# RWKV element stage of a two-layer encoder trunk: ten chunks at once on VectorE, b and k of both heads packed, 64x64 products, inverses of two head pairs together

## The chip, the cores and the metric

One core of a Trainium2 chip (trn2) runs the whole program. The metric is device time in microseconds: the median of several executions. One more execution is recorded by the hardware profiler; its span, from the first to the last instruction, is what the rows below are counted in.

## The reference

The kernel computes one inference step of a trunk of two layers (width 1024) in float32: an even layer with a pooling mixer and differential attention, an odd layer with RWKV-7 time mixing, in both layers cross attention and SwiGLU behind the mixer, and a final norm. There are 512 tokens of a prompt and 8 sequences of 16 tokens of a sample, 640 columns together. What matters here is the recurrence of the odd layer, for 16 heads of size 64:

```
kk = heads(k * k_k); kk = kk / max(norm(kk), 1e-12)
k  = k * (1 + (a - 1) * k_a);  decay = exp(-exp(w))
def step(S, inp):
    r_t, d_t, k_t, v_t, kk_t, a_t = inp
    sa = einsum('bhvk,bhk->bhv', S, -kk_t)
    S = S * d_t + sa[..., None] * (kk_t * a_t) + v_t[..., None] * k_t
    return S, einsum('bhvk,bhk->bhv', S, r_t)
xs = (r, decay, k, v, kk, a) over time
S_fin, y = lax.scan(step, S0, xs)
```

## The kernel before, in words

Features lie on the partitions and the 640 tokens on the free axis; a tile of 128 features holds two heads, a head pair `m` (0 to 7). Large products (`block_steps`, written by `mm`, line 224) split weights and inputs into a high and a low part and take three products of 128x128 weights with 320 columns for each block. `load_w` makes the parts: ScalarE rounds (`wh`, line 241), VectorE or GpSimd subtracts (`wl`).

SBUF is cut into 59 numbered slots of 656 columns (kind `t`) and 22 of 256 (`n`), PSUM into 8 banks; a tile that takes a slot waits for the work on that slot alone. All `dma_start` calls of the RWKV stage except a few outputs are issued by SyncE, one queue in program order. The order of instructions on each engine is made by the framework's scheduler, which runs the program in a timeline simulation and goes by priorities; the priorities follow the order in which the code is written.

The recurrence is computed in chunks of 64 tokens (8 chunks of the prompt, 2 of the sample). For every head pair `rw_elem` makes from the projections `k`, `r` and the low-rank inputs the running decay (`up`, line 1452, a scan), its reciprocal `pi`, the in-context rate `am`, the normed key `kn`, and of these `zr` = (-kk P(t-1) | r P) and `bk` = (b = kk a / P | k (1 + (a-1) k_a) / P), all as [128 features, chunk, 2, 64]. `zr` lies in two tiles of five chunks (a ring of three), `bk` in two tiles a head and five chunks each, where the rows of the other head hold zeros (three sets, `bks`). VectorE writes `zr` in eight instructions and the `b` half of `bk` in four; GpSimd multiplies `kn` by `am`, `am` by `k`, and writes the `k` half of `bk` in four. Then come, for groups of four, four and two chunks, the products (b | k)^T (z | r) with 128x128 weights (line 1510), masked by VectorE into `gm` and stored by SyncE into the DRAM scratch `d_gb` and `d_w` (lines 1514 and 1515); `zr` goes to `d_w` (line 1501), and the transposes of `bk` (line 1524) go over ScalarE (line 1526) to `d_bt` (line 1527).

`inverse` (one head pair) reads 16x16 blocks back from `d_gb` with eight DMAs (line 1539), inverts them, one block on each of 80 partitions, in a loop of 15 steps of one multiplication and one sum on VectorE (lines 1547 and 1548), stores them (line 1549), reads them back in another layout, and joins them to 32x32 and 64x64 blocks with small products into `p_l` and VectorE and ScalarE steps, down to `mt` (lines 1597 to 1600). Its temporaries are one buffer each, so a loop ends before the next pair's blocks are loaded.

Between these steps `pace` puts pieces of a large product as a filler: the rest of the receptances for the first pairs, then the values (`gemm_tok_steps`). `elem` starts the first part of the next pair (to the `yield`) ahead of the second part of the present one. When all eight pairs are done, `chunk` runs the chunks of two groups of four pairs, each hanging on the state of the one before, with `sample`, `y_norm` and the gates between them.

Of the kernel before, what the change touches and what calls it, by code (L numbers as in the profile page):

```python
# [9 lines left out]
F32 = mybir.dt.float32  # L10
# [16 lines left out]
NSLOT = 59  # L27
# [3 lines left out]

class Held(list):
    """tiles that stay until they are given back"""
# [3 lines left out]
class Trunk:  # L37
    """The tiles of SBUF and PSUM lie in numbered slots of one size, a tag each, so that what waits for
    a slot waits for the work on that slot alone. Slots are taken the longest free first."""
# [5 lines left out]
    XV = 9  # L45
# [9 lines left out]
    IB = [1, 1, 1, 1]  # L55
# [29 lines left out]
    def ring(self, kind, name, n, dt):  # L85
        """a temporary: the next of the n slots that the name has in this scope"""
# [123 lines left out]
    def split(self, hl, src, scale=None, eng=None):  # L210
        """hl = the two float32r parts of src (times a per-partition scale)."""
# [20 lines left out]
    def load_w(self, src, kb, cols, rows=128):  # L232
        """src: DRAM view [rows, kb, cols], or pieces ((c0, c1), view) of one; returns its float32r parts."""
# [34 lines left out]
    def gemm(self, hl, w2d, ncols, evac, r0=0, c0=0, halves=HALVES, first=()):  # L268
        """first: parts of the first blocks of weights, when they are there already"""
# [11 lines left out]
    def gemm_tok(self, hl, w2d, c0, ncols, ntiles, evac, nb=None):  # L281
        """tokens on the partitions, two tiles of them a bank, nb banks at once: evac(i, c, psum [128, 256])"""
# [26 lines left out]
    def constants(self):  # L309
# [15 lines left out]
        # rows (h, m, t) -> (h, t)  # L325
# [3 lines left out]
        # selectors of partition bits: bit 16  # L329
# [3 lines left out]
        # sequence selector of rows s (mod 64) // 16  # L333
# [3 lines left out]
        # heads of a pair: features to head rows and back  # L337
# [4 lines left out]
        # iota on the free dim and row index  # L342
# [7 lines left out]
        # masks of the chunk: [strict | inclusive]  # L350
# [8 lines left out]
        # reciprocal counts of the first positions  # L359
# [3 lines left out]
        # the scan starts anew behind each of these columns  # L363
# [5 lines left out]
    def columns(self):  # L369
        """vectors over features as columns"""  # L370
# [38 lines left out]
        # lambda  # L409
# [11 lines left out]
        # 1 on the rows of the first map, -lambda on those of the second  # L421
# [14 lines left out]
    def load_x(self):  # L436
        """the transposes follow in turn_x"""
# [33 lines left out]
    def rms(self, role, pool=True):  # L471
        """1 / rms of the tokens: [128, 5] with tokens on the partitions, and as rows on all partitions"""
# [26 lines left out]
    def normed(self, gcol):  # L499
        """float32r parts of x * gain; 1 / rms is applied behind the product"""  # L500
# [10 lines left out]
    def even(self):  # L511
# [48 lines left out]
        # scores of the samples' new keys, a column block a sequence  # L560
# [8 lines left out]
        # outputs: new keys and values  # L569
# [18 lines left out]
        with self.scope():  # L588
            # history of the pool
# [87 lines left out]
    def softmax_rows(self, p, s, name):  # L677
        """exp(s - max) into p, returns 1 / sum"""
# [8 lines left out]
    def diff_prompt(self, h, q, k, vt, out):  # L687
        """one head of the prompt: out [128, (token tile, e)], normalised by the first map's sum"""
# [3 lines left out]
        for i in range(4):  # L692
# [20 lines left out]
            # p0 - lambda p1, over the sum of p0  # L713
# [12 lines left out]
    def sub_ln(self, tiles, name):  # L726
        """groups of 128 columns of the tiles [128, 512], in place: over their rms"""
# [1194 lines left out]
```

## Time and profile before

| | |
|---|---|
| median of 3 runs | 2436.52 us (2433.37 to 2438.97) |
| span of the profiled execution | 2428.2 us; the page gives no other time of it |
| TensorE matmuls, share of the span | 94% |
| VectorE, ScalarE, GpSimd | 53%, 34%, 22% |
| DMA | 280.42 MB, mean 115 GB/s |

Busy time is time in which an engine executes an instruction; issues of DMAs, waits and semaphores are not counted. Matmuls are pipelined and their ends modelled, so the sum of a group's durations is more than its busy time. A float32 matmul with both operands unrounded is recorded as two. Some matmul records are missing from a trace. The granted TensorE clock is 1.00 at 2.4 GHz and 0.50 at 1.2 GHz; a stretch between has had some of both. A line of the code can be a helper's: all plain elementwise products of VectorE and GpSimd have line 205, those with a scalar 208, all matmuls but transposes 224.

### The profile page before, as it was taken

The page shows a single profiled execution, that of the slowest core. Times are in us where ns is not written, and L with a number is a line of the kernel's source. Part 1 is how long each engine was busy: PE and PEld are TensorE (multiplying, and loading weights), DVE is VectorE, ACT ScalarE, POOL GpSimd, SP SyncE. Part 2 cuts the span into 40 slices and gives each one's busy share as a digit, 9 for nine tenths or more (in the row PEclk, how much of TensorE's full clock was granted, in tenths as well). Part 3 has the DMA queues.
Part 4 walks back from the last instruction along what each step waited for, and adds up shares of the span by engine and source line. Part 5 has one row for each costly group of instructions (what it writes and reads, how often), then busy time and mean ns, then how long its engine had stood idle before and what let it go on. Part 6 is the DMA issues. An engine that isn't in the chain of part 4 may idle for free. (4 is left out here: it accounts for less than half of the span.)

```text
span 2428.2 us, 45754 instructions
## 1 busy us (share of the span) xinstructions
PE 2281.2 (94%) x18943; PEld 2119.8 (87%) x18943; DVE 1284.7 (53%) x2361; ACT 814.5 (34%) x1493; POOL 525.4 (22%) x536
## 2 busy tenths in 40 slices
PE   8998999999999999979998987696999999999998
PEld 7886999789999999978887876574997899999997
DVE  4467543454434424484759886579444544344344
ACT  4335432333212212366734432222323432122122
POOL 2122220012101102244555322233200212011010
PEclk9999999999999999999997878797999999999999
DMA  3218644423222222453245556674445222222222
GB/s 120 74 62 295 204 136 148 160 77 87 74 75 79 71 87 73 135 163 91 74 128 149 145 138 157 183 204 118 135 132 165 65 79 72 77 79 81 76 72 77
DMA packets 428322, 280.42 MB, mean 115 GB/s; under 512 B 79130, under 2 KB 383535, under 8 KB 428114
## 3 DMA queue, kind: packets, MB, share of 16 engines
q1 hardware_dynamic: 424513, 268.01, 38.0%
q0 software_dynamic: 3600, 9.49, 1.1%
q8 instruction: 149, 2.44, 0.4%
q14 instruction: 60, 0.48, 0.1%
HBM read 231.22 MB, written 46.20 MB: 114 GB/s over the span
## 5 line engine op out<-in xcount | busy, mean ns | idle before, releaser
L224 PE MATMUL p_g<-xn,wh 128*128 128x320 f32 x3712 | 721.6, 310 | 0.4 <-DVE xn L208 0.4
L224 PEld LDWEIGHTS p_g<-xn,wh 128*128 128x128 f32 x3712 | 588.7, 188 | 9.8 <-issue 8.4
L241 ACT CAST wh<-wr 128x1024 fp32r<-128x1024 f32 (+3 forms) x279 | 272.8, 978 | 861.7 <-PE p_g L224 534.0
L224 PE MATMUL p_g<-xn,wl 128*128 128x320 f32 x1856 | 444.1, 310 | 3.3 <-DVE wl L205 3.3
L205 DVE TENSOR_TENSOR wl<-wr,wh 128x1024 fp32r<-128x1024 f32 (+2 forms) x251 | 305.6, 1218 | 73.9 <-ACT wh L241 57.2
L224 PEld LDWEIGHTS p_g<-xn,wl 128*128 128x128 f32 x1856 | 316.2, 188 | 7.0 <-DVE wl L205 3.7
L224 PE MATMUL p_g<-hid,wh 128*128 128x320 f32 x1408 | 264.8, 309 | 0.0
L205 POOL TENSOR_TENSOR gate<-gate,sgate 128x320 f32<-128x320 f32 x88 | 118.1, 1363 | 676.1 <-DVE gate L205 517.6
L205 DVE TENSOR_TENSOR gate<-p_g,rstd 128x320 f32<-128x320 f32 x176 | 78.3, 486 | 327.5 <-PE p_g L224 324.8
L205 DVE TENSOR_TENSOR x<-x,p_g 128x320 f32<-128x320 f32 x192 | 85.5, 483 | 281.6 <-PE p_g L224 281.5
L224 PEld LDWEIGHTS p_g<-hid,wh 128*128 128x128 f32 x1408 | 221.4, 188 | 0.0
L224 PE MATMUL p_g<-hid,wl 128*128 128x320 f32 x704 | 161.4, 310 | 0.0
L224 PE MATMUL p_g<-mixr,wh 128*128 128x320 f32 (+2 forms) x640 | 128.4, 313 | 3.1 <-ACT wh L241 2.6
L224 PEld LDWEIGHTS p_g<-hid,wl 128*128 128x128 f32 x704 | 117.6, 188 | 0.0
L224 PE MATMUL p_g<-xohl,wh 128*128 128x320 f32 x512 | 110.0, 319 | 4.8 <-ACT xohl L214 4.7
L224 PEld LDWEIGHTS p_g<-mixr,wh 128*128 128x128 f32 (+2 forms) x640 | 98.5, 179 | 11.6 <-issue 5.6
L205 POOL TENSOR_TENSOR acc<-acc,sq 128x640 f32<-128x640 f32 x36 | 66.2, 1840 | 146.3 <-ACT sq L202 146.1
L224 PEld LDWEIGHTS p_g<-xohl,wh 128*128 128x128 f32 x512 | 82.4, 188 | 9.9 <-ACT xohl L214 7.0
L948 POOL TENSOR_SCALAR xp<-xp,xsm 128x256 f32<-128x256 f32 x32 | 15.3, 478 | 305.6 <-DVE xsm L684 299.6
L224 PE MATMUL p_g<-mixr,wl 128*128 128x320 f32 (+2 forms) x320 | 78.0, 314 | 0.0
L205 POOL TENSOR_TENSOR wl<-wr,wh 128x1024 fp32r<-128x1024 f32 (+2 forms) x28 | 64.4, 2301 | 60.4 <-ACT wh L241 57.2
L205 DVE TENSOR_TENSOR hid<-gate,hid 128x320 fp32r<-128x320 f32 x88 | 72.1, 819 | 7.8 <-ACT hid L214 7.8
(485 smaller groups left out, 3836.4 us busy)
## 6 DMA issues: line engine op xcount, KB each, us to landing
wr<-in_ffn_wg SPq DMA_DIRECT2D x44, 512.0 KB
wr<-in_ffn_wu SPq DMA_DIRECT2D x44, 512.0 KB
kc<-in_cache_mem_k SPq DMA_DIRECT2D x64, 256.0 KB
vc<-in_cache_mem_v SPq DMA_DIRECT2D x64, 256.0 KB
wr<-in_ffn_wd SPq DMA_DIRECT2D x32, 512.0 KB
wr<-in_ev_w_in SPq DMA_DIRECT2D x16, 512.0 KB
wr<-in_xa_wk SPq DMA_DIRECT2D x16, 512.0 KB
kc<-in_cache_diff_k SPq DMA_DIRECT2D x32, 256.0 KB
```

Of the source, the lines that this page charges most:

```text
L205: (eng or self.nc.vector).tensor_tensor(out, a, b, op=op)
L224: self.nc.tensor.matmul(out, lhsT, rhs, start=start, stop=stop, **kw)
L241: nc.scalar.copy(wh[0:rows, 0:n], wr[0:rows, 0:n])
L948: nc.gpsimd.tensor_scalar(p, p, rs, 1.0, op0=ALU.mult, op1=ALU.mult)
```

## The change

- The elementwise part of a head pair works over all ten chunks at once. `zr` and `bk` are one tile of 1280 columns each, two buffers each of their own (`wide`), outside the numbered slots. `zr` takes four instructions; the products of `kn`, `am`, `k` and `pi` are four instructions of VectorE over 128x640; GpSimd has none of them.
- `bk` holds b and k of both heads without zeros. Each product of a chunk is four matmuls of 64x64 weights: head `h` reads partitions 64h.., and half `e` (b or k) writes the PSUM rows `half(h, e)`.
- `zr` is stored by two DMAs instead of four; `bt` by nine instead of three, as the second head's halves come out in the other order.
- The second part of the low-rank products and the key direction's product take 128 rows with zeros in place of 64 rows (`wz`, two tiles; two `rn` tiles, one a group).
- `inverse` takes two head pairs: sixteen loads of blocks, one loop over [80, 2, n, n], joins of 16 chunks. It follows every odd pair.
- The numbered slots go from 59 to 56, the ring of `vc` in the cross attention from 9 to 8 tiles, GpSimd's DMA scratch to 4096. The inverses of the first group are given back after its last chunk.

```diff
-NSLOT = 59
+NSLOT = 56
+BACC = dict(dynamic_dma_scratch_size=4096)
-    XV = 9
+    XV = 8
+    def wide(self, tag, name):
+        return self.sb.tile([128, 1280], F32, tag=tag, name=name, bufs=1)
...
-            yield from self.rw_elem(m, r, k, rns[0][0][f, 0:NT], selT[m % 4 // 2][0][f, c:c + 128], low_in, sp)
+            yield from self.rw_elem(m, r, k, rns[m // 4][0][:, 0:NT], selT[m % 4 // 2][0][:, c:c + 128], low_in, sp)
...
-            inv[m] = self.inverse(m, sp, nsv[m // 4][:, m % 4])
+            if m % 2:
+                inv[m - 1:m + 1] = self.inverse(m - 1, sp, [nsv[i // 4][:, i % 4] for i in (m - 1, m)])
...
+        wz = self.wz[m % 2]
+        for i in range(2):
+            r = slice(64 * i, 64 * i + 64)
+            nc.scalar.copy(wz[r, i * 128:(i + 1) * 128], ws[r, i * 128:(i + 1) * 128])
...
-            self.mm(p[:, 0:n], wa[r, i * 128:(i + 1) * 128], low[2][r, t0:t0 + n], start=False, stop=True)
+            self.mm(p[:, 0:n], wz[:, i * 128:(i + 1) * 128], low[2][:, t0:t0 + n], start=False, stop=True)
...
-        self.stt(zr[0][:, :, 0, :], ch(kn[:, 0:320]), -1.0, P[:, 0:5, 0:64])
-        self.stt(zr[1][:, 0:3, 0, :], ch(kn[:, 320:512]), -1.0, P[:, 5:8, 0:64])
-        self.tt(zr[0][:, :, 1, :], ch(r_[:, 0:320]), P[:, 0:5, 1:65])
-        self.tt(zr[1][:, 0:3, 1, :], ch(r_[:, 320:512]), P[:, 5:8, 1:65])
...
+        self.stt(zr[:, 0:8, 0, :], ch(kn[:, 0:512]), -1.0, P[:, :, 0:64])
+        self.tt(zr[:, 0:8, 1, :], ch(r_[:, 0:512]), P[:, :, 1:65])
+        self.stt(z4(0), s4(kn[:, 512:640]), -1.0, p4(S[:, :, 0:16]))
+        self.tt(z4(1), s4(r_[:, 512:640]), p4(S[:, :, 1:17]))
...
-        self.tt(kn, kn, am, eng=nc.gpsimd)
+        self.tt(kn, kn, am)
         self.act(am, am, AF.Identity, scale=c1("rw_k_a"), bias=self.ka1[:, m:m + 1])
-        self.tt(am, am, k, eng=nc.gpsimd)
-        for i in range(2):
-            for h in range(2):
...
-                self.tt(bk[i][h][r, :, h, :], ch(kn[r, s]), ch(pi[r, s]))
-                self.tt(bk[i][h][r, :, 1 - h, :], ch(am[r, s]), ch(pi[r, s]), eng=nc.gpsimd)
+        self.tt(bk[:, :, 0, :], ch(kn), ch(pi))
+        self.tt(am, am, k)
+        self.tt(bk[:, :, 1, :], ch(am), ch(pi))
...
+        half = lambda h, e: slice(64 * (e ^ h), 64 * (e ^ h) + 64)
...
-                for h in range(2):
-                    i = (c0 + c) // 5
-                    self.mm(pg[h][:, c * 128:(c + 1) * 128], piece(bk[i][h], c0 + c), piece(zr[i], c0 + c))
+                for e in range(2):
+                    for h in range(2):
+                        self.mm(pg[h][half(h, e), c * 128:(c + 1) * 128], bk[hs(h), c0 + c, e, :],
+                                zr[hs(h), c0 + c].rearrange("p z t -> p (z t)"))
...
-            nc.sync.dma_start(out=sp["bt"][c0:c0 + nch, :, m, :].rearrange("c p f -> p c f"), in_=bt)
+                for src, dst in ((half(0, 0), half(1, 0)), (half(0, 1), half(1, 1))) if h else ((slice(0, 128), slice(0, 128)),):
+                    nc.sync.dma_start(out=sp["bt"][c0:c0 + nch, dst, m, f].rearrange("c p f -> p c f"), in_=bt[src, :, f])
...
-            t = T[:, 0:n * n].rearrange("p (t j) -> p t j", t=n)
-            self.tt(t, Nv[:, s + 1:16, s + 1:16].rearrange("p j t -> p t j"), Xv[:, s, s + 1:16].unsqueeze(1).to_broadcast([nb, n, n]))
-            nc.vector.tensor_reduce(Nv[:, s, s + 1:16], t, axis=AX.X, op=ALU.add)
+            t = T[:, 0:2 * n * n].rearrange("p (i t j) -> p i t j", i=2, t=n)
+            self.tt(t, Nv[:, :, s + 1:16, s + 1:16].rearrange("p i j t -> p i t j"),
+                    Xv[:, :, s, s + 1:16].unsqueeze(2).to_broadcast([nb, 2, n, n]))
+            nc.vector.tensor_reduce(Nv[:, :, s, s + 1:16], t, axis=AX.X, op=ALU.add)
```

## Rows read from the trace of the kernel before

**Rows 1.** The page: the span, and busy us and share by engine.

```profile
span 2428.2 us, 45754 instructions
...
PE 2281.2 (94%) x18943; PEld 2119.8 (87%) x18943; DVE 1284.7 (53%) x2361; ACT 814.5 (34%) x1493; POOL 525.4 (22%) x536
```

**Rows 2.** Busy us by stretch: PE, PEld, DVE, ACT, POOL, granted clock, DMA share, GB/s.

```profile
1205.00:1275.00 70.00, 69.79 (x493) 62.36 (x492) 39.27 (x67) 28.09 (x53) 37.35 (x36) 1.00 0.45 119
1275.00:1475.00 200.00, 173.63 (x2107) 150.99 (x2105) 169.75 (x389) 78.97 (x172) 79.31 (x91) 0.81 0.57 144
...
1500.00:1660.00 160.00, 130.27 (x2334) 102.73 (x2334) 103.38 (x235) 41.97 (x103) 37.06 (x31) 0.84 0.71 199
```

**Rows 3.** Instructions of three lines: ns min/median/max, first and last start us, shapes.

```profile
L1452 DVE TENSOR_TENSOR_SCAN u<-rst,u x8: 1510/1522/3210, 1215.7 to 1443.1; 128x656 f32<-128x656 f32 x8
...
L1549 SPq DMA_DIRECT2D d_np<-in x8: 329/430/522, 1309.7 to 1517.4; - x8
...
L1600 ACT COPY mt<-p_l x16: 344/362/363, 1337.8 to 1536.6; 32x256 f32<-32x256 f32 x16
```

**Rows 4.** Waits of PE, 1275 to 1475 us, the longest: us, times, longest.

```profile
PE p_f L224 <- DVE kn L208: 7.4, 5, 3.7
```

**Rows 5.** DVE groups, 1205 to 1540 us (busy us, mean ns), and one of `rn`.

```profile
L205 DVE TENSOR_TENSOR bk<-kn,pi 64x320 f32<-64x320 f32 x32 | 30.1, 941 | 3.8 <-POOL kn L205 3.3
...
L205 DVE TENSOR_TENSOR it<-in,ix 80x225 f32<-80x225 f32 x8 | 4.3, 538 | 0.2
...
L1548 DVE TENSOR_REDUCE in<-it 80x15 f32<-80x225 f32 x8 | 3.0, 376 | 0.1
...
L205 DVE TENSOR_TENSOR it<-in,ix 80x1 f32<-80x1 f32 x8 | 1.2, 147 | 5.3 <-DMA ix<-d_gb 3.5 <-DMA d_v<-vtok 1.4 <-issue 0.4
L1548 DVE TENSOR_REDUCE in<-it 80x1 f32<-80x1 f32 x8 | 1.2, 146 | 0.2
...
L205 DVE TENSOR_TENSOR rn<-krst,rn x2: 816/819/822, 1153.6 to 1198.2; 32x640 fp32r<-32x640 f32 x2
```

**Rows 6.** DVE alone, 1205 to 1540 us: sums for `zr`, then for the loops.

```profile
sum 335.00, DVE 21.83; mean DVE 7.28
...
sum 335.00, DVE 77.59; mean DVE 25.86
```

**Rows 7.** POOL groups, 1205 to 1540 us: busy us, mean ns, idle before.

```profile
L205 POOL TENSOR_TENSOR bk<-am,pi 64x320 f32<-64x320 f32 x32 | 33.4, 1045 | 2.4
L205 POOL TENSOR_TENSOR wl<-wr,wh 128x1024 fp32r<-128x1024 f32 x14 | 33.2, 2376 | 30.2 <-ACT wh L241 27.0 <-PE p_g L224 3.0
L205 POOL TENSOR_TENSOR kn<-kn,am 128x640 f32<-128x640 f32 x8 | 12.4, 1551 | 34.1 <-DVE zr L208 25.1 <-DVE in L1548 8.9
```

**Rows 8.** The timeline of DVE and of POOL: start us, us, instructions merged.

```profile
1327.08 4.98 DVE L205 TENSOR_TENSOR bk<-kn,pi 64x320 f32<-64x320 f32 x4
...
1328.54 4.25 POOL L205 TENSOR_TENSOR bk<-am,pi 64x320 f32<-64x320 f32 x4
```

**Rows 9.** PE groups, 1205 to 1540 us; last, `p_e` alone by stretch.

```profile
L224 PE MATMUL p_f<-zr,bk 128*128 128x128 f32 x320 | 56.9, 335 | 1.1 <-DVE gm L205 1.0
...
L224 PE MATMUL p_g<-mixr,wh 128*128 128x320 f32 x226 | 48.6, 317 | 0.2 <-DVE krst L194 0.2
...
1275.00:1475.00 200.00, 25.10 (x54) 0.81 0.57 144
```

**Rows 10.** PE groups, 1500 to 1660 us: busy us, mean ns, idle before.

```profile
L224 PE MATMUL p_c<-u,mt 64*64 64x64 f32 x240 | 13.6, 234 | 0.5 <-ACT mt L1600 0.5
...
L224 PE MATMUL p_x<-S,wcs 64*32 64x128 f32 x256 | 10.5, 300 | 0.3 <-ACT S L192 0.3
```

**Rows 11.** Issues on SyncE's queue: ns min/median/max, first and last start us.

```profile
L1539 SPq DMA_DIRECT2D ix<-d_gb x64: 739/756/972, 1261.6 to 1501.2; - x64
...
L1501 SPq DMA_DIRECT2D d_w<-zr x32: 575/626/791, 1233.8 to 1461.8; - x32
...
L1527 SPq DMA_DIRECT2D d_bt<-am x16: 364/536/1399, 1262.6 to 1491.0; - x16
```

More of the change, by code (lines that the diff above doesn't have):

```diff
@@ L54 @@
     CP = '01s01sn01s01sn0101Gn01Y01n'
-    IB = [1, 1, 1, 1]
     AH = 1
@@ L1291, in rwkv @@
         self.banks(g=(0, 1), f=(2, 3, 4, 5), l=(6,), e=(7,))
-        bks = self.take(6, "bk")
-        self.bk = [[t[:, 0:NT] for t in bks[2 * i:2 * i + 2]] for i in range(3)]
-        for b in self.bk:
-            for h in range(2):
-                nc.gpsimd.memset(b[h][64 - 64 * h:128 - 64 * h], 0.0)
+        wzs = self.take(2, "wz", "n", dt=F32R)
+        self.wz = wzs
+        for t in wzs:
+            nc.gpsimd.memset(t[64:128, 0:128].bitcast(F32), 0.0)
+            nc.gpsimd.memset(t[0:64, 128:256].bitcast(F32), 0.0)
         with self.scope():
@@ L1323, in step @@
                     todo.append((g, c // 2))
+                if c == 7 and g == 0:
+                    self.give(*inv[0:4])
             if self.CV < 8:
@@ L1396, in rwkv @@
         self.give(*yh)
-        self.give(*inv, ns)
+        self.give(*inv[4:8], ns)
         yo = self.hl(8, "yo")
@@ L1533, in inverse @@
         nb = 80
-        X, N = [self.n(nm, self.IB[0])[0:nb] for nm in ("ix", "in")]
-        T = self.n("it", self.IB[1])[0:nb]
-        for b in range(8):
-            h, q = b // 4, b % 4
-            r = slice(64 * h + 16 * q, 64 * h + 16 * q + 16)
-            nc.sync.dma_start(out=X[b:nb:8].rearrange("c (s t) -> c s t", s=16), in_=sp["gb"][:, r, m, 16 * q:16 * q + 16])
+        X, N, T = [self.t(nm, 1)[0:nb, 0:512] for nm in ("iX", "iN", "iT")]
+        for i in range(2):
+            for b in range(8):
+                h, q = b // 4, b % 4
+                r = slice(64 * h + 16 * q, 64 * h + 16 * q + 16)
+                nc.sync.dma_start(out=X[b:nb:8, 256 * i:256 * i + 256].rearrange("c (s t) -> c s t", s=16),
+                                  in_=sp["gb"][:, r, m + i, 16 * q:16 * q + 16])
@@ L1557, in inverse @@
-        mt = self.take(1, "mt")
-        M = mt[0][:, 0:512].rearrange("p (c t) -> p c t", c=8)
+            t = T[:, 0:2 * n * n].rearrange("p (i t j) -> p i t j", i=2, t=n)
+            self.tt(t, Nv[:, :, s + 1:16, s + 1:16].rearrange("p i j t -> p i t j"),
+                    Xv[:, :, s, s + 1:16].unsqueeze(2).to_broadcast([nb, 2, n, n]))
+            nc.vector.tensor_reduce(Nv[:, :, s, s + 1:16], t, axis=AX.X, op=ALU.add)
+        n16 = self.n("n16", 1)
+        gz, mts = [], []
+        for i in range(2):
+            nc.sync.dma_start(out=sp["np"][m + i].rearrange("c b s t -> (c b) (s t)"), in_=N[:, 256 * i:256 * i + 256])
+            nv = sp["np"][m + i].rearrange("c b s t -> (b s) c t")
+            nc.sync.dma_start(out=n16[:, 128 * i:128 * i + 128].rearrange("p (c t) -> p c t", c=8), in_=nv[:, 0:8])
+            nc.sync.dma_start(out=ns[i], in_=nv[:, 8:10])
+            gz.append(self.t("gz")[:, 0:512].rearrange("p (c t) -> p c t", c=8))
+            nc.sync.dma_start(out=gz[i], in_=sp["gb"][0:8, :, m + i, 0:64].rearrange("c p f -> p c f"))
+            mts.append(self.take(1, "mt"))
@@ L1574, in inverse @@
+        Y = NI
+        self.tt(Y, p, NI, ALU.subtract)
         p = self.ps("l")
-        for c in range(8):
+        for c in range(16):
             for r in quads:
                 self.mm(p[r, o(c)], Y[r, o(c)], N[r, o(c)])
-        self.tt(T, N, p[:, 0:256], ALU.add)
+        T = N
+        self.tt(T, N, p, ALU.add)
         tt_, Y2 = NT_, Y
@@ L1582, in inverse @@
         p = self.ps("l")
-        for c in range(8):
+        for c in range(16):
             for h in range(2):
                 a, b_ = quads[2 * h], quads[2 * h + 1]
-                self.mm(p[b_, o(c)], gz[a, c, 32:64], tt_[a, o(c)], tile_position=(64 * h, 64 * h + 32))
+                self.mm(p[b_, o(c)], gz[c // 8][a, c % 8, 32:64], tt_[a, o(c)], tile_position=(64 * h, 64 * h + 32))
         for h in range(2):
             b_ = quads[2 * h + 1]
-            nc.scalar.copy(Y2[b_], p[b_, 0:256])
+            nc.scalar.copy(Y2[b_], p[b_])
         p = self.ps("l")
-        for c in range(8):
+        for c in range(16):
             for h in range(2):
```

96 lines of the change are left out of this document (43 added, 53 removed).

## The prediction

> **What bounds the kernel now.** I read the shares of the span first, then the busy time by stretches. TensorE is busy 94% of the 2428.2 us [rows 1], so outside one part nothing but fewer matmuls could shorten the kernel. That part is the RWKV mixer. Up to 1275 us its element stage runs under TensorE work without a gap: 69.79 of 70 us busy, clock 1.00. From 1275 to 1475 TensorE is busy 173.63 of 200 us with a granted clock of 0.81, that is, a good part of the stretch at 1.2 instead of 2.4 GHz, while VectorE is busy 169.75 of 200 us and GpSimd 79 [rows 2]. No engine is full; each waits on the others in turn. The head pairs follow each other at a steady pace: the scan (one a pair) starts at 1215.7 and for the eighth time at 1443.1 us, so a period is 227.4 / 7 = 32.5 us [rows 3]. The longest wait of TensorE here is for `kn`, which VectorE makes [rows 4]. The chain of waits of the whole kernel covers only its last microseconds and says nothing of this stage.
>
> Why VectorE is slow is seen when its rows are held against GpSimd's. A quarter-product of `bk` on VectorE takes 941 ns in the mean, though it has 64x320 elements and one of 32x640 needs 819 [rows 5]. In the timeline four of them last 4.98 us beside four of GpSimd lasting 4.25 [rows 8]: the two engines take turns, and one waits while the other has two inputs in SBUF. GpSimd's elementwise steps of this stage (`bk` 33.4 us, `kn` 12.4, and two `am` groups that I take as long as `kn`'s) thus are paid for by VectorE as well [rows 7].
>
> **VectorE's part of the change.** Four products of 128x640 a pair replace four quarter-products and GpSimd's six instructions: 8 x 4 x 0.82 = 26.2 us, where `bk` took 30.1 before [rows 5]: -3.9 us. The `zr` operands take four instructions in place of eight, over 512 and 128 columns; two of them I price as one of 640 plus 0.15 us for the second start (the one-element row of the loop): 16 x 0.97 = 15.5 against 21.8 us [rows 5, 6]: -6.3 us. The loop of the 16x16 inverses runs once for two pairs. Its multiplication costs 147 ns at 1 element and 538 at 225, its sum 146 and 376 [rows 5], so about 145 ns for each start and 1.74 and 1.03 ns an element. The 15 steps hold 1240 elements: 15 x 0.29 + 1240 x 0.00277 = 7.8 us for a pair, and for two at once 4.35 + 6.9 = 11.2 us. Eight singles would be 62 us and four doubles 45: -17 us. The loops took 77.6 us, though [rows 6]; the other 15 us I put down to turns with GpSimd. GpSimd loses some 58 us of two-input work and keeps `wl` (33.2 us) and about 10 us of `mixr`, so 6 of the 15 stay: -9 us. Together VectorE loses 36 us over eight pairs, 28 of the 200 us stretch (200 / 260 of the stage). The steps after the loop (transposes, subtractions at double width) I leave at their cost; a gain there is not counted. Two small ScalarE copies a pair lie on an engine that is busy 79 of 200 us [rows 2]; without that cover they would be 16 x 0.3 = 5 us.
>
> **TensorE's part.** The products of `zr` and `bk` were 160, recorded as 320 passes of 128x128 by 128 columns in 56.9 us [rows 9]; now they are 640 passes of 64x64. No row shows that shape. From below: 64x32 blocks with 128 columns took 10.5 / 256 = 41 ns each, which gives 26 us, -31 us. From above: 64x64 blocks with 64 columns took 13.6 / 240 = 57 ns; twice that for 128 columns gives 73 us, +16 us [rows 10]. The value taken is 47 us, -10 us, as the 64x32 row has the same columns and inputs but four column groups where 64x64 has two. The low-rank and key-direction products become full 128x128. In the stretch the 54 of them took 25.10 us, 465 ns each, while the same 320 columns cost 48.6 / 226 = 215 ns in `mixr`'s products [rows 9]; for 80 of them about -17 us (some run at the higher clock). As `zr`'s products now lie in quadrants between filler matmuls, I charge 24 groups with one such change in and out, 0.25 us each: +6 us. Sum: -21 us busy, -16 in the stretch; bounds -42 and +5 for the whole.
>
> The last two items may be held against the Trainium skill. "TensorEngine Tiling (Array Packing)", Key Properties, says that changing the tiling mode drains the array, and that tiles work independently, four of them at 64x64. The 465 against 215 ns agree with the drain, and it speaks against the products' quadrants; four free tiles would give a quarter of the passes' time, 2 x 56.9 / 4 = 28 us, near the lower end above. Without the drain the sum would be 6 us better.
>
> **SyncE's part.** DMA issues are not counted as busy, but the queue is in order. `zr` leaves in 2 DMAs of ten chunks instead of 4; an issue is 0.63 us whatever its size here, so -1.25 us a pair. `bt` leaves in 9 DMAs instead of 3: 6 x 0.54 = +3.2 us [rows 11]. So SyncE gets 2 us more a pair, 16 in all, and behind it wait the loads of the inverses. If each step is hidden by the waits that the queue has anyhow, it costs 0; if the queue is what ends last, 16 us. I take a third, +5 us. Loads of weights stand in the same queue.
>
> **The rest.** One slot less for `vc` delays one load at each of eight calls of the cross attention, at most an issue of 0.76 us each, 6 us; I take 0, since other loads are under way. Fewer slots, the smaller scratch of GpSimd's DMAs and the memsets lie under TensorE's work; no row prices them, and I keep +5 us for them in the range.
>
> **The tail.** The inverses are a chain: the last three store their blocks as the queue lets them, the last at 1517.4, and the last copy of an inverse comes at 1536.6 us [rows 3]. Now the last loop starts only when pair 7 has landed, for pairs 6 and 7 together: 16 issues of 0.76 us = 12 us instead of 6 behind it, a loop of 11 instead of 8 us, wider steps after; against that the inverse of pair 6 no longer stands before it. I take +2 us, between -10 and +14; chunks of the first group go on meanwhile.
>
> **The sum.** TensorE loses 16 and VectorE 28 of 200 us; as neither is full, I let the stretch shrink by their mean, 22 us, 11%. Over 260 us (eight periods) that is -28.6. With +5 for SyncE and +2 for the tail the change is -22, and -4 for the shorter chain of the last pair, whose GpSimd steps (`kn`, `am`, `bk`, some 7 us) become some 3 us of VectorE: -26 us. The span goes to 2402 us. The median of the runs, 2436.52, lies 8.3 us above the profiled span; the page has no other time for that execution, so I carry these 8.3 us over: 2410 us.
>
> **The rivals.**
> 1. VectorE and GpSimd's turns are the whole bound: then the stage follows VectorE's 28 of 200 us, 14% or 36 us of 260, and with denser TensorE the clock of 0.81 rises; a tenth of the 174 us back is 14 us. 2436 - 50 = 2386. For it: the taking of turns [rows 8], the wait for `kn` [rows 4]. Against: TensorE has the higher share [rows 2].
> 2. SyncE's queue sets the period: it gets 2 us more a pair, and what VectorE gains is waited for there. Then 2436, from -4 to +4. For it: 8 issues of 0.76 us for each inverse, and more than twenty other issues a pair. Against: TensorE's waits name VectorE.
> 3. Slower: the tail pays. The last inverse of two pairs waits for pair 7 and SyncE's 16 issues, the second group's chunks start later by up to 14 us, and the paired loop holds VectorE for 11 us at a time in each of four places, which delays `gm` and `kn` by 3 to 4 us each, 14 us in all; with half the stage's gain gone too (-14): 2436 + 14 = 2450. It decides where the last copy of an inverse comes more than 14 us behind its place relative to the last `gm` of before. For it: behind the last pair there are no more filler products of the values. Against: the loops of before are interleaved with other work.
> 4. The quadrants don't overlap: products +16 instead of -10 us, of which the stage shows half: 2423.
>
> **How the numbers follow.** Forecast 0.50, rival 1 0.17, rival 2 0.13, rival 3 0.13, rival 4 0.07. A measurement of this kernel can tell about 0.2%, 5 us, from no change. Faster: 0.48 + 0.17 + 0.07 + 0.03 = 0.75; same: 0.02 + 0.08 = 0.10; slower: 0.13 + 0.02 = 0.15. The forecast's own range is 2396 to 2426. The range for all reaches from 2380 (rival 1 with the lower product price) to 2440, leaving out most of rival 3.
>
> **What would show it.** Right: the scans' period falls from 32.5 to about 29 us; the products `bk` on VectorE last 0.8 us each with no instruction of GpSimd beside them; loops sum to about 50 us; `p_e` products cost 0.2 us instead of 0.465; the second stretch's clock rises over 0.81. Wrong: a period of 32 us with SyncE's issues back to back (rival 2); the last copy of an inverse no earlier than 1536 us (rival 3); the products over 57 us (rival 4); a change of more than 5 us outside 1205 to 1700 us.

## The result, and the profile after

The changed kernel takes 2512.27 us in the median of 4 runs (2501.18 to 2519.75), beside 2435.22 us for the kernel before: a ratio of 1.032 with an interval of 1.0291 to 1.0348. The forecast was 2410 us, faster; it is 77 us slower. The profiled execution took 2501.18 us, 1.8 us more than its span.

The page of the changed kernel: the span, and busy us and share of each engine.

```profile
span 2499.4 us, 46250 instructions
...
PE 2362.7 (95%) x19263; PEld 2148.2 (86%) x19263; DVE 1249.0 (50%) x2181; ACT 820.2 (33%) x1501; POOL 467.1 (19%) x484
```

TensorE is busy 81.5 us longer than in [rows 1], while VectorE and GpSimd have less to do, as meant. The same stretches as in [rows 2], changed kernel:

```profile
1205.00:1275.00 70.00, 64.45 (x446) 56.48 (x445) 34.30 (x48) 26.07 (x50) 21.73 (x21) 0.93 0.36 97
1275.00:1475.00 200.00, 194.00 (x1787) 132.75 (x1785) 109.71 (x211) 70.53 (x148) 30.59 (x47) 0.61 0.49 121
1500.00:1660.00 160.00, 126.60 (x2103) 103.30 (x2104) 83.22 (x171) 36.39 (x85) 22.30 (x27) 0.75 0.57 148
```

From 1275 to 1475 us TensorE is now busy 194 of 200 us, yet it starts 1787 matmuls where there were 2107, and its granted clock is 0.61 instead of 0.81. VectorE went from 169.75 to 109.71 us of 200: it waits more than before. Scan and last copy of an inverse, as in [rows 3]:

```profile
L1463 DVE TENSOR_TENSOR_SCAN u<-rst,u x8: 1508/1518/2242, 1209.3 to 1499.9; 128x656 f32<-128x656 f32 x8
...
L1619 DVE COPY mt<-p_l x16: 401/417/422, 1378.2 to 1621.0; 32x256 f32<-32x256 f32 x16
```

The period of the head pairs is (1499.9 - 1209.3) / 7 = 41.5 us, not 29. Two TensorE groups and `bk`, 1205 to 1600 us (busy us, mean ns, idle before):

```profile
L230 PE MATMUL p_g<-wh,mixr 128*128 128x256 f32 x320 | 104.0, 396 | 1.7 <-ACT mixr L220 1.1 <-POOL mixr L211 0.6
L230 PE MATMUL p_f<-zr,bk 64*64 64x128 f32 x640 | 95.7, 385 | 5.2 <-DVE gm L211 3.0 <-DVE zr L211 1.9 <-DVE bk L211 0.2
...
L211 DVE TENSOR_TENSOR bk<-am,pi 128x640 f32<-128x640 f32 x8 | 8.6, 1079 | 0.2
L211 DVE TENSOR_TENSOR bk<-kn,pi 128x640 f32<-128x640 f32 x8 | 6.6, 824 | 0.2
```

The products of `zr` and `bk`, forecast at 47 us, take 95.7 (56.9 in [rows 9]). Where it goes is seen in TensorE's timeline of the changed kernel (start us, us, instructions merged; the time of one reaches into the next), with the stretch's busy us by engine and its granted clock (0.50) under it. A float32 product is two matmuls in the records, so each `x2` is one quadrant product:

```profile
1370.21 0.58 PE L230 MATMUL p_g<-wl,mixr 128*128 128x256 f32 x1
1370.72 0.69 PE L230 MATMUL p_f<-zr,bk 64*64 64x128 f32 x2
1371.34 0.58 PE L230 MATMUL p_g<-wh,mixr 128*128 128x256 f32 x1
1371.85 0.69 PE L230 MATMUL p_f<-zr,bk 64*64 64x128 f32 x2
1372.46 0.58 PE L230 MATMUL p_g<-wh,mixr 128*128 128x256 f32 x1
```

```profile
1369.00:1382.00 13.00, 13.00 (x103) 7.85 (x102) 4.08 (x9) 2.87 (x6) 0.00 (x0) 0.50 0.29 71
```

One full-width matmul of the filler stands between every two quadrant products, and a round of three matmuls takes 1371.85 - 1370.72 = 1.13 us, with no idle time, at 1.2 GHz. In the order of the records from 1190 to 1600 us the 640 matmuls of the products lie in 131 unbroken runs, 90 of them of just two, and the tile shape changes 417 times between successive matmuls; in the kernel before the 320 matmuls of the products lie in 39 runs, and there are 293 changes.

### The profile page after: what moved, and what is told of

Its sections match the earlier page's. It is cut to its first block, busy times and chain, and to the rows that moved or that the text cites. A ratio compares the mean times of both kernels' runs of the same rounds, so it can differ in the third digit from the quotient of the medians.

```text
span 2499.4 us, 46250 instructions
## 1 busy us (share of the span) xinstructions
PE 2362.7 (95%) x19263; PEld 2148.2 (86%) x19263; DVE 1249.0 (50%) x2181; ACT 820.2 (33%) x1501; POOL 467.1 (19%) x484
## 5 line engine op out<-in xcount | busy, mean ns | idle before, releaser
L230 PE MATMUL p_g<-wh,mixr 128*128 128x256 f32 x320 | 104.0, 396 | 1.7 <-ACT mixr L220 1.1
L230 PE MATMUL p_f<-zr,bk 64*64 64x128 f32 x640 | 95.7, 385 | 5.2 <-DVE gm L211 3.0
L230 PEld LDWEIGHTS p_g<-wh,mixr 128*128 128x128 f32 x320 | 71.0, 253 | 23.4 <-issue 17.9
```

Source lines behind the costliest of these rows:

```text
L230: self.nc.tensor.matmul(out, lhsT, rhs, start=start, stop=stop, **kw)
```

## The experiments

All ratios are to runs of the kernel before on the same chip; medians of different rows may come from different chips, so that differences between rows are best taken from the ratios. The last column is the mean granted clock from 1200 to 1520 us of the profiled execution.

| kernel | median us | ratio (95%) | clock |
|---|---|---|---|
| before | 2431 to 2435 | 1 | 0.85 |
| changed | 2512.27 | 1.0320 (1.0291 to 1.0348) | 0.68 |
| quad_only | 2488.96 | 1.0236 (1.0221 to 1.0252) | 0.66 |
| grouped | 2484.14 | 1.0214 (1.0199 to 1.0229) | 0.73 |
| before_grouped | 2497.98 | 1.0265 (1.0238 to 1.0293) | 0.78 |
| mid_dose | 2455.69 | 1.0101 (1.0086 to 1.0116) | 0.79 |
| quad_hp | 2464.37 | 1.0132 (1.0107 to 1.0158) | 0.74 |
| before_hp | 2435.90 | 1.0011 (0.9998 to 1.0024) | 0.82 |
| half_tiles | 2453.80 | 1.0086 (1.0068 to 1.0105) | 0.75 |
| half_tiles_hp | 2461.14 | 1.0120 (1.0101 to 1.0138) | 0.77 |
| full_tiles | 2446.43 | 1.0072 (1.0052 to 1.0091) | 0.82 |
| full_single | 2454.07 | 1.0099 (1.0084 to 1.0115) | 0.81 |
| warm_hp | 2445.57 | 1.0078 (1.0052 to 1.0103) | 0.82 |
| full_bt | 2414.49 | 0.9927 (0.9911 to 0.9943) | 0.84 |
| hp_bt | 2445.76 | 1.0053 (1.0038 to 1.0068) | 0.82 |
| half_bt | 2453.11 | 1.0080 (1.0063 to 1.0097) | 0.76 |
| after_bt | 2483.63 | 1.0202 (1.0182 to 1.0222) | 0.73 |
| before_split | 2451.97 | 1.0069 (1.0044 to 1.0094) | 0.83 |
| full_bt_warm | 2418.28 | 0.9928 (0.9908 to 0.9949) | 0.88 |
| full_bt_single | 2444.06 | 1.0036 (1.0024 to 1.0049) | 0.84 |

**The quadrants alone, on the kernel before** (quad_only):

```diff
...
-                for h in range(2):
-                    i = (c0 + c) // 5
-                    self.mm(pg[h][:, c * 128:(c + 1) * 128], piece(bk[i][h], c0 + c), piece(zr[i], c0 + c))
+                i = (c0 + c) // 5
+                for e in range(2):
+                    for h in range(2):
+                        self.mm(pg[h][64 * (e ^ h):64 * (e ^ h) + 64, c * 128:(c + 1) * 128],
+                                bk[i][hs(h), (c0 + c) % 5, e ^ h, :], piece(zr[i], c0 + c, hs(h)))
...
```

> The kernel before with one part of the change alone: b and k packed and the products of a chunk as four 64x64 matmuls; GpSimd's steps, zr's halves, the low-rank products, the stores and the single inverses stay. In its built order 320 products stand in 91 runs between filler matmuls and the tile shape changes 404 times in the element stage (208 in the kernel before, 399 in the changed one). Theory A (each change between 64x64 and 128x128 drains TensorE, some 0.2 us and more, and the drained array falls to 1.2 GHz): 2475 to 2515 us, clock of the stage under 0.7. Rival B (the paired inverse and its tail cost the 75 us): within 10 us of 2436. Rival C (SyncE's longer queue): within 10 us of 2436. Rival D (64x64 passes are slow by themselves): 2475 or more, as A.

+2.4%, 57 us of the 77. So the quadrants bring most of the loss with none of the other parts there. Theory A and rival D forecast the same here; the next runs part them.

**The products kept together.** In grouped and before_grouped each group of products stands in a critical section of the planner, in mid_dose it only has a priority over the fillers:

```diff
+            with self.tc.tile_critical():          # grouped; before_grouped: around the 128x128 products
+            with self.tc.high_priority(1000):      # mid_dose
                 for c in range(nch):
...
```

> The changed kernel with nothing else than the order: the products of each group of four or two chunks stand together, with no filler matmul among them. 320 products in 19 runs, 125 changes of tile shape instead of 399. Theory A: the loss goes and the savings of the other parts appear, 2385 to 2425 us, clock of the stage over 0.8. Rival B: still 2490 to 2515. Rival C: still 2490 to 2515. Rival D: 2480 or more.

> Control: the kernel before, its 128x128 products held together in the same way (23 runs instead of 39, 171 changes of tile shape instead of 208, most of them from other products). Theory A: the products have the filler's own shape, so little changes: 2425 to 2440. If grouping alone is worth something whatever the shape: under 2425.

> The changed kernel with the products given a higher priority in the order but not held together: 43 runs, 200 changes of tile shape, between the 125 of the grouped one and the 399 of the changed one. Theory A: by the number of changes between the two, nearer to the grouped one: 2400 to 2440. Rivals B and C: 2490 to 2515.

Both sections missed: the control, with no quadrant in it, lost 2.65%. TensorE's waits in grouped, 1205 to 1520 us (us, times, longest), tell why:

```profile
PE p_f L230 <- DMA iX<-d_gb: 16.8, 5, 6.4
...
PE p_f L230 <- DMA ws<-in_rw_w: 7.5, 1, 7.5
PE p_f L230 <- DMA kr1spill<-krst: 5.1, 2, 2.9
```

The products read none of `iX`, `ws` and `kr1spill`: by these waits the section waits for work of the other queues too. Those two runs thus say nothing on the quadrants. The priority does. In mid_dose the products lie in 62 runs, and 57 of the 77 us come back, though not down to theory A's 2440. Its products (the row as above), and its timeline in two stretches, with the clock of both:

```profile
L230 PE MATMUL p_f<-zr,bk 64*64 64x128 f32 x640 | 52.2, 325 | 22.4 <-DVE gm L211 9.4 <-DVE bk L211 5.9 <-ACT am L1535 4.2
```

```profile
1339.59 1.97 PE L230 MATMUL p_f<-zr,bk 64*64 64x128 f32 x14
...
1342.15 1.97 PE L230 MATMUL p_f<-zr,bk 64*64 64x128 f32 x16
...
1374.87 0.63 PE L230 MATMUL p_g<-wh,mixr 128*128 128x256 f32 x2
1375.29 0.41 PE L230 MATMUL p_g<-wl,mixr 128*128 128x256 f32 x1
```

```profile
1339.00:1344.00 5.00, 5.00 (x97) 4.14 (x86) 1.29 (x2) 0.27 (x1) 0.00 (x0) 0.50 0.40 73
1374.00:1378.00 4.00, 4.00 (x23) 3.60 (x23) 1.61 (x5) 1.35 (x3) 1.01 (x2) 0.50 0.35 72
```

Also at 1.2 GHz, but among its like, a quadrant matmul costs 1.97 / 16 = 0.12 us and a filler matmul (1375.29 - 1374.87) / 2 = 0.21. So quadrants aren't slow by themselves (rival D). Two and one are 0.45 us, against the 1.13 us of the round above: 0.68 us for one change in and out. The changed kernel has the same round at 2.4 GHz (granted clock 1.00 from 1403 to 1409 us):

```profile
1407.87 0.43 PE L230 MATMUL p_f<-zr,bk 64*64 64x128 f32 x2
1408.22 0.38 PE L230 MATMUL p_g<-wl,mixr 128*128 128x256 f32 x1
1408.54 0.43 PE L230 MATMUL p_f<-zr,bk 64*64 64x128 f32 x2
```

It takes 1408.54 - 1407.87 = 0.67 us, and 0.63 in the mean of the eleven such rounds at this clock. Among their like a filler matmul of this shape costs 0.12 us there and a quadrant matmul 0.04 (the run of 42 from 1385.4 us of mid_dose), so two and one 0.20: 0.43 us for a change in and out. With 131 runs that is 56 to 89 us. The trace also shows what is missing in a round: the weight load of the filler matmul of 1371.34 starts together with it (1371.333 and 1371.335 us), where among its like it starts one matmul ahead (mid_dose: load at 1374.870, its matmul at 1375.081).

**The priority on the other bases, and half as many, wider tiles.** quad_hp and before_hp put the same priority on quad_only and on the kernel before. half_tiles replaces the quadrants of the changed kernel by one product of 64x128 a head, half_tiles_hp adds the priority:

```diff
-                for e in range(2):
-                    for h in range(2):
-                        self.mm(pg[h][half(h, e), c * 128:(c + 1) * 128], bk[hs(h), c0 + c, e, :],
+                for h in range(2):
+                    self.mm(pg[h][:, c * 128:(c + 1) * 128], bk[hs(h), c0 + c].rearrange("p z t -> p (z t)"),
...
```

> The kernel before with the quadrant products as its only change, now issued in long runs (a priority for each group of products, so that the filler matmuls of the projections fall between groups: 41 runs of products in the built order of the element stage, 91 without the priority). Theory S (the loss is in the changes of tile shape): the loss of 54 us over the kernel before shrinks with the runs, to 0 to 15 us, so 2430 to 2446, and 1300 to 1500 us has a granted clock like that of the kernel before (0.82 to 0.85). Theory K (narrow products leave TensorE at 1.2 GHz even in long runs): 2447 to 2465, with under 0.78 in that stretch. Theory L (the rest of the 25 us that the grouped change still loses comes from its other parts): at most 2435.

> Control: the kernel before with the same priority for its own 128x128 products and nothing else changed. All theories: the priority itself is worth little, 2425 to 2440. If it comes out over 2445, the priority costs by itself and the grouped variants understate what the long runs give; if under 2420, long runs help whatever the tile shape.

> The changed kernel with one edit: b and k of a head and chunk go through TensorE as one 64x128 product (320 products, the two heads in the two halves of the rows) instead of two 64x64 quadrants (640); everything else of the change is kept. 211 changes of tile shape in the built order of the element stage (399 in the changed kernel, 208 in the kernel before). Theory S: the time follows the changes, so the loss of 77 us goes and some of the gain that was forecast shows, 2400 to 2430. Theory K: products half as narrow, half of the clock's loss stays, 2440 to 2475. Theory L: the other parts cost 25 us, 2450 to 2465.

> The same with the priority for each group of products. Theory S: within 8 us of the variant without it, as its changes of tile shape are nearly as many (205 against 211). Theory K: 5 to 20 us below it, as the products then come in denser runs. Theory L: as without it.

The priority costs nothing that can be told on the kernel before (before_hp). quad_hp and half_tiles came out where theory K put them; half_tiles_hp is 7 us over half_tiles and so misses K's forecast of less; it lies where S and L had it. Half tiles have fewer changes of shape than the kernel before (274 in the records, 293 there) and stay 0.9% slower at a clock of 0.75. That alone doesn't refute theory S, since the other parts of the change are there too: beside full_tiles (below), which has them with 128x128 products, half_tiles is 0.14% slower, within the intervals. quad_hp, at 2464 us, lies over the ranges of S (2446 at most) and L (2435 at most): on the kernel before grouped quadrants still cost 1.3%.

**The quadrants undone, and dense work added.** full_tiles has 128x128 products over zeros and all the rest of the change, but for `bk`, which is held once instead of twice and written by four instructions; full_single also single inverses; warm_hp is mid_dose with two full-width products ahead of each group, which the quadrants overwrite:

```diff
-        self.tt(bk[:, :, 0, :], ch(kn), ch(pi))                           # full_tiles; the same for am, 1
+        for h in range(2):
+            self.tt(bk[h][hs(h), :, 0, :], ch(kn[hs(h)]), ch(pi[hs(h)]))
...
-                        self.mm(pg[h][half(h, e), c * 128:(c + 1) * 128], bk[hs(h), c0 + c, e, :],
+                    self.mm(pg[h][:, c * 128:(c + 1) * 128], bk[h][:, c0 + c].rearrange("p z t -> p (z t)"),
...
-                inv[m - 1:m + 1] = self.inverse(m - 1, sp, [nsv[i // 4][:, i % 4] for i in (m - 1, m)])   # full_single
+            inv[m] = self.inverse(m, sp, nsv[m // 4][:, m % 4])
...
+                for p in pg:                                              # warm_hp
+                    self.mm(p[:, 0:nch * 128], wa[:, 0:128], low[0][:, 0:nch * 128])
```

> The changed kernel with its quadrants alone undone: b and k of a head lie over zeros again and the products are 320 of 128x128, all other parts of the change kept (wide operands, element steps on the vector engine, full-width low-rank products, paired inverses); the zero-padded operands are held once, not twice, and their four writes a pair take 64 partitions each (some 1.6 us of the vector engine a pair more). 128 changes of tile shape in the built order of the element stage (399 in the changed kernel, 208 in the kernel before). Theory Q (the whole loss comes from the quadrants, by their changes of shape and by the low clock that goes with them; the other parts gain what was forecast for them or some of it): 2395 to 2425, and under 100 us at the lower clock between 1200 and 1520 us (208 in the changed kernel, 96 in the kernel before). Theory L (the other parts lose 25 us by themselves): 2445 to 2465.

> The same with the inverses of single pairs, as in the kernel before, in place of the paired ones. Theory Q with the forecast's terms: 9 us a two pairs of vector time come back, some of it hidden: 0 to +15 us on the variant with pairs. Rival 3 (the pairing lengthens the tail): 5 to 15 us under it.

> The changed kernel with the priority for each group of products, and with work added: ahead of each group's quadrants two float32r products of 128x128 over the group's columns go to the same banks, which the quadrants then overwrite (48 products, 20,480 columns, some 9 us of TensorE by the 0.2 us that a 512-column one takes at full clock). 231 changes of tile shape in the built order (200 without the added products). Theory K (the loss that is left after grouping is the clock that narrow products let fall; dense work among them holds it up): not slower than without the added work, 2440 to 2456, and less time at the lower clock between 1200 and 1520 us than 147 us. Theory W (the added low-clock time is only where the work happens to lie; TensorE's work sets the end): 2460 to 2475, with 147 us or more.

full_tiles came out in theory L's range, not Q's: something besides the quadrants costs. It isn't the pairing, as single inverses are 8 us slower still. warm_hp adds work to TensorE and, as theory K had it, is not slower, with a clock of 0.82 instead of 0.79 (its profiled execution is the fastest of the four, 2438.40 us); its ratio lies under that of mid_dose, but the intervals overlap.

**The stores.** The changed kernel stores the transposed `b` and `k` in nine pieces a pair, so that one order of `b` and `k` serves both heads. full_bt, hp_bt, half_bt and after_bt go back to three, on full_tiles, mid_dose, half_tiles and the changed kernel; before_split does the reverse to the kernel before:

```diff
-                for src, dst in ((half(0, 0), half(1, 0)), (half(0, 1), half(1, 1))) if h else ((slice(0, 128), slice(0, 128)),):
-                    nc.sync.dma_start(out=sp["bt"][c0:c0 + nch, dst, m, f].rearrange("c p f -> p c f"), in_=bt[src, :, f])
+            nc.sync.dma_start(out=sp["bt"][c0:c0 + nch, :, m, :].rearrange("c p f -> p c f"), in_=bt)
...
-        self.tt(bk[:, :, 0, :], ch(kn), ch(pi))
+        for h in range(2):
+            self.tt(bk[hs(h), :, h, :], ch(kn[hs(h)]), ch(pi[hs(h)]))
...
```

> The changed kernel with two parts undone: the quadrants (128x128 products over zeros, as in full_tiles) and the split stores of the transposed b and k (one store of 512-byte rows a group again, 3 a pair, instead of three of 256-byte rows, 9 a pair); head 1's b and k are written in the order k, b for it, by the same four writes. Theory T (the split stores cost: ScalarE's next copy waits for the store before it, 26 us of such waits in the grouped variant, and SyncE's list grows): 2420 to 2438, so 8 to 26 us under full_tiles (2446). Theory U (full_tiles is slow for another reason: its zero-padded operands are held once, and TensorE waited 14 us for them): within 6 us of full_tiles.

> The changed kernel with its quadrants, the priority for each group of products, and the stores of the transposed b and k undivided as above (b and k in four writes of 64 partitions a pair). Theory T: 8 to 26 us under the same kernel with split stores (2456), so 2430 to 2448, still over the kernel before, by what the quadrants leave. Theory U: 2450 to 2465.

> The changed kernel with 64x128 products in place of the quadrants and the undivided stores, no priority; b and k held twice. Theory T: 8 to 26 us under half_tiles (2454), 2428 to 2446. Theory U: 2450 to 2460.

> The changed kernel with the split stores alone undone (three stores of 512-byte rows a pair, b and k in four writes of 64 partitions); the quadrants stay and no priority is given. With the changed kernel (2512), full_tiles (2446) and full_bt (2414) it makes a table of two by two. If the two causes add, 2475 to 2490, and the quadrants cost 60 to 75 us with either kind of store. If the stores cost only where TensorE has room (with quadrants it sets the end anyway), within 10 us of 2512.

> The kernel before with the split stores as its only change: the same bytes, but 9 stores a pair of 256-byte rows in place of 3 of 512-byte rows. Theory T: 10 to 32 us slower than the kernel before, 2441 to 2463. If the stores cost only beside the change's other parts: 2428 to 2438.

full_bt gained more than theory T gave: 32 us on full_tiles, and at 2414.49 us it is 0.73% under the kernel before, so faster than both kernels. hp_bt (10 us under mid_dose) and before_split came out in T's ranges, after_bt in the range for two causes that add. With these the two causes stand in a table; its last two columns are ScalarE's waits for `ws` and for the stores (`d_bt`), summed from 1205 to 1500 us:

| products | nine stores | three stores | waits, nine | waits, three |
|---|---|---|---|---|
| quadrants (changed, after_bt) | 1.0320 | 1.0202 | 38.0 | 17.1 |
| 128x128 over zeros (full_tiles, full_bt) | 1.0072 | 0.9927 | 40.8 | 30.3 |
| quadrants with the priority (mid_dose, hp_bt) | 1.0101 | 1.0053 | 37.2 | 25.6 |
| 64x128 (half_tiles, half_bt) | 1.0086 | 1.0080 | 31.5 | 37.2 |
| of the kernel before (before_split, before) | 1.0069 | 1 | 44.0 | 9.9 |

In the first two rows the quadrants cost 2.5 to 2.75% (60 to 67 us), the split stores 1.2 to 1.45% (29 to 35 us), and they add. In the next two rows they don't: there the split costs 0.5% and nothing that can be told, and beside 128x128 the shape costs 0.3% and 0.14% with nine stores, but 1.3% and 1.5% with three. before_split shows the stores by themselves, +0.69%, 17 us; its edit is the first of the diff above, the other way round. half_bt does not follow theory T (1 us under half_tiles): it is also the one kernel in which three stores don't shorten ScalarE's waits. How the stores cost is seen in before_split on SyncE's queue and ScalarE around one wait:

```profile
1400.85 1.88 SPq L1529 DMA_DIRECT2D d_bt<-am  x3
1402.77 1.28 SPq L1529 DMA_DIRECT2D d_bt<-pi  x2
...
1408.51 6.75 SPq L1541 DMA_DIRECT2D ix<-d_gb  x8
...
1416.32 1.19 SPq L1426 DMA_DIRECT2D ws<-in_rw_w  x2
1417.55 1.53 SPq L1426 DMA_DIRECT2D ws<-in_rw_a  x2
```

```profile
1421.46 0.40 ACT L1427 CAST wa<-ws 128x256 fp32r<-128x256 f32 x1 [15.51 <-DMA ws<-in_rw_a]
```

The queue issues without a gap over 0.4 us from 1395 to 1425 us. The nine pieces take 1.88 + 1.28 + 0.57 + 0.56 + 1.24 = 5.5 us of it; behind them the loads of `ws` for the next pair, 32 KB each, are issued from 1416.3, and ScalarE, which needs them for `wa`, stands still for 15.51 us with all that is queued behind. The waits from 1205 to 1500 us (us, times, longest), of the kernel before and then of before_split:

```profile
ACT wa L1427 <- DMA ws<-in_rw_a: 0.5, 1, 0.5
...
PE p_e L224 <- DVE wa L205: 3.5, 1, 3.5
```

```profile
ACT wa L1427 <- DMA ws<-in_rw_a: 23.6, 3, 15.5
...
PE p_e L224 <- DVE wa L205: 7.0, 3, 4.4
```

So ScalarE waits 23 us longer for `ws`, of which 3.5 us reach TensorE as a wait for `wa`; how the rest of the 17 us comes about isn't shown. Nor are the stores all that stands before `ws` there: so do the eight loads `ix`, 6.75 us, where the kernel before issues the first half of `ws` ahead of them:

```profile
1402.24 1.17 SPq L1426 DMA_DIRECT2D ws<-in_rw_w  x2
...
1406.78 1.67 SPq L1539 DMA_DIRECT2D ix<-d_gb  x2
```

The planner orders the whole program anew with every edit: the products, which before_split doesn't touch, lie in 56 runs there instead of 39. What such a new order costs by itself no run parts from what its edit costs, so differences of ten or twenty us between two single rows stay uncertain; the quadrants' 57 to 67 us were found on three bases.

**The controls of the clock and of the paired inverses.** full_bt_warm adds warm_hp's two products a group to full_bt; full_bt_single has full_single's edit on full_bt.

> Control for warm_hp: full_bt with the same two added float32r products of 128x128 ahead of each group of products (48 in all, some 9 us of TensorE), where the products fill the array already. Theory K: nothing is gained here, 2416 to 2428. If added work makes this one faster as well (under 2410), the gain in warm_hp is one of order, not of the clock with quadrants.

> full_bt with the inverses of single pairs, as in the kernel before. The forecast's term (9 us of vector time less for two pairs with pairing, 26 us of loops in all over four, part of it hidden): 3 to 12 us slower than full_bt, 2417 to 2427. Rival 3 (the pairing lengthens the tail): 2400 to 2412, and then this is the version to keep.

The added work costs and gains nothing that can be told where there are no quadrants. Single inverses cost 27 to 30 us (by the ratios and by the medians), more than any theory gave: the pairing is worth having here. VectorE's loops take 20.6 us more with them (72.0 against 51.4).

## Why the prediction was wrong, step by step

**The failed step** is in TensorE's part: "I charge 24 groups with one such change in and out, 0.25 us each: +6 us". The price was low (0.43 us at 2.4 GHz, 0.68 at 1.2), and the count was wrong by far: the planner puts fillers between the products of a group, and they lie in 131 runs, not 24. What the quadrants cost is 60 to 67 us, where the forecast had -4 for products and changes together. Already before the change the products lay in 39 runs, which its timeline could have told. [Rows 9] held the warning, too: each of the `p_e` matmuls at 465 against 215 ns had a neighbour of another shape, and the forecast used that as a gain for 80 matmuls but not as a price for 640.

**The products** at 47 us would have been nearly right for products left together: 52.2 us in mid_dose, at a mean clock of 0.79. Rival 4 (quadrants that don't overlap) had a mark, over 57 us, that is met, for another reason: quadrants among their like are not slow, the changes are.

**The clock** was taken to rise. It fell to 0.61 in the second stretch, while TensorE was never idle for long (1.9 us at most from 1200 to 1520 us). At two levels, a mean of 0.68 from 1200 to 1520 us means (1 - 0.68) / 0.5 x 320 = 205 us at 1.2 GHz, before 96; work that fills those 109 us would need half at 2.4 GHz, some 54 us of the 60 to 67. That is the same loss seen from the other side, not one to be added: the changes cost more where the clock is low. What lowers it isn't settled. Quadrants go with a lower clock (0.68 against 0.82 with nine stores, 0.73 against 0.84 with three), half tiles too (0.75, 0.76); where full-width products were added it was higher (warm_hp), with intervals of the time that overlap. But ahead of the falls TensorE did not run quadrants alone: in the 4 us before the longest one, at 1286.8 us, it ran 33 matmuls of 64x64 with one column (`ones`, `kn`, which the kernel before has, too), two or three quadrants and 8 full-width matmuls, with no idle time; before the one at 1355.0 us no quadrant, but 72 matmuls of 32x32 and 26 of 64x64. Grouped quadrants cost 0.3% with nine stores (mid_dose against full_tiles) and 1.3% with three (hp_bt against full_bt, clocks of 0.82 and 0.84, hp_bt's from an execution 10 us under its median); this remainder is open.

The Trainium skill, "TensorEngine Tiling (Array Packing)", Key Properties, says that a change of mode drains the array; the 0.43 to 0.68 us of a change in and out fit that, though no run parts a drain from a weight load that no longer starts ahead.

**SyncE's part** is the second term that failed. It was +16 us of issues, 26 for the split stores less 10 for `zr`, of which a third was charged, +5. The split stores alone measured 29 to 35 us with the change's other parts and 17 on the kernel before. The issues were counted rightly (0.58 to 0.6 us each now), but "if each step is hidden by the waits that the queue has anyhow" doesn't hold where the queue runs back to back, as in the stretch above. Rival 2 named this mechanism and gave it only the gain to eat. The smaller rows may have a share: 256-byte packets took the page's count under 512 B from 79,130 to 100,377 in before_split. The Trainium skill, "DMA: Bandwidth & Descriptors", Specifications, asks for 512 bytes or more for the full rate; no run here parts that from the number of issues.

**VectorE's part** held in the main. Busy us from 1205 to 1600 us, changed kernel, loops and then `zr`; the same of full_bt, and last the loops of full_bt_single:

```profile
1205.00:1600.00 395.00, 48.09 (x120) 0.69 0.47 119
...
1205.00:1600.00 395.00, 19.99 (x32) 0.69 0.47 119
```

```profile
1205.00:1600.00 395.00, 51.39 (x120) 0.85 0.60 159
...
1205.00:1600.00 395.00, 15.50 (x32) 0.85 0.60 159
...
1205.00:1600.00 395.00, 71.98 (x240) 0.84 0.57 148
```

The loops were forecast at 51 us, `zr` at 15.5 (19.99 in the changed kernel), and `bk` at 0.82 us each (0.824 and 1.079). But the stage was to shrink by the mean of TensorE's and VectorE's savings, and with TensorE busy 194 of 200 us it went by TensorE alone: VectorE waited, and its gain bought nothing that shows. Only part of the 15 us in the loops was turns with GpSimd: single loops without GpSimd's steps still take 72.0 us (full_bt_single) of the 77.6 in [rows 6].

**The low-rank products** came to 427 ns (20.07 us for 47) at the clock of 0.61, and to 352 in full_bt (19.73 for 56), not 215. Some 9 of the 17 us came. So the change of shape was not their whole price: in full_bt 30 of the 56 have no neighbour of another shape and 25 have one, where before 37 of 54 had two and 17 one. What keeps them at 352 ns is open.

**The tail.** Rival 3's mark was met: the last copy of an inverse comes 76.7 us behind the start of the last `gm` (1544.3), 50.9 before. But in full_bt, with the same pairing, it is 50.9 again (1475.4 to 1526.3), and single inverses are slower. So the pairing by itself isn't the cause.

**What was left of the forecast** is full_bt: without quadrants and split stores the change gives -18 us, where -26 were forecast. Its scans and its stretches:

```profile
L1466 DVE TENSOR_TENSOR_SCAN u<-rst,u x8: 1506/1518/2877, 1207.8 to 1426.1; 128x656 f32<-128x656 f32 x8
...
1205.00:1275.00 70.00, 67.00 (x447) 62.39 (x447) 37.44 (x50) 27.43 (x54) 23.71 (x21) 0.93 0.38 104
1275.00:1475.00 200.00, 167.85 (x2248) 151.89 (x2248) 160.43 (x297) 83.47 (x176) 39.23 (x58) 0.83 0.62 159
```

2248 matmuls in the second stretch instead of 2107, in less busy time: that is the gain. The pairs' period is (1426.1 - 1207.8) / 7 = 31.2 us, where 29 were forecast and 32.5 were before. That the total comes near the forecast is no proof of its sum: full_bt has neither the quadrants' -4 us nor the +5 for SyncE, and its `bk` takes VectorE 31.5 us in four writes a pair, not two of 0.82 us.

## What to carry to other kernels

A smaller tile shape is priced by the number of times that the order of the work changes shape, and this number is read from the order in which the planner lays the changed program, or at the least from the timeline of before (39 runs, and 131 after), not from the number of groups; where full-width fillers are put between, keep the products of one shape together or leave them wide over zeros. A DMA added to a queue that issues back to back is not hidden because it is small: here 26 us of issues cost between nothing and 35 us, so look for the loads behind it and for who waits for them. When a change has several parts, make the table of two by two of the suspects early: here it took the parts that gain out of a kernel that loses.

## What was not expected of the hardware

TensorE was recorded busy 194 of 200 us and had a granted clock of 0.61: here a high busy share did not go with 2.4 GHz. A change between 128x128 and 64x64 and back cost 0.43 us at 2.4 and 0.68 us at 1.2 GHz. 64x64 matmuls of 128 columns followed each other every 41 ns at 2.4 GHz in a run of 42 (mid_dose, from 1385.4 us), so 640 of them alone would be 26 us, the lower bound of the forecast.
